# A hybrid decoder layer on one core: the decay columns of the first half in column strips, and the last level of the block inverses in quarters of the array

## The chip, the core and the metric

The kernel runs on one core of a Trainium2 chip. The metric is the device time of one execution in microseconds (us); lower is better. TensorE is called PE here, with its weight loads (PEld) shown apart; VectorE is DVE, ScalarE is ACT, GpSimd is POOL, and SyncE (SP) issues most DMAs.

## What is computed

One layer on 1024 tokens of width 2048: a combined input projection, three groups of heads, one output projection, a final RMSNorm. The part that the change touches is group B, the gated DeltaNet with 8 heads of 128. Cut to what matters:

```python
h = rmsnorm(x, ln_g)
proj = h @ w_in                      # d_a, d_b: 8 + 8 columns among 6672
g = -exp(dn_a_log) * softplus(d_a + dn_dt_bias)   # log decay per head and token
beta = sigmoid(d_b)
# per head, per chunk of the tokens
g_cum = cumsum(g)
a = strict_lower((k * beta) @ k.T * exp(g_cum_i - g_cum_j))
T = inverse(I + a)                   # unit lower triangular
v_new = T @ (beta * v) - T @ (beta * k * exp(g_cum)) @ state
```

All large products are made to nearly fp32 accuracy: each operand is split into a high and a low part in the one-pass type fp32r, and three products of the parts are added. Plain fp32 products take two PE instructions each.

## The kernel before

Tokens are worked in two halves of 512 (four tiles of 128). `h`, transposed, stands in SBUF as `ahi` and `alo` (16 row blocks k of 128 features by 512 tokens, four to a tile `q`). Weights come as pieces through `wraw` and are split into `whi` (ACT cast) and `wlo` (DVE subtraction). A product of 128 columns of `w_in` with a half is 48 matmuls of 128x512.

The order of every engine's instructions is made before anything is issued: `Plan.add` (lines 138 to 186) records each operation with its dependences, `Plan.price` gives it a cost, and `Plan.issue` (229 to 300) lets each engine take the ready operation of the lowest rank, then the oldest. Matmuls recorded in `together()` stay side by side. After a group with more than 7 followers, line 296 adds 250 ns to PE's planned time. `behind(op)` makes operations wait for `op` in the plan. All instructions carry line 300, so the trace is read by tiles.

- **Opening (lines 489 to 674).** The memory tokens' keys and values, and between them `prep(tt, put, bank)` for the tiles of the first half: scale a tile's rows (`row_scale`: four squares on ACT into `jk` and `small`, then POOL's power), transpose on PE, and `put0` (579 to 593), which splits the transposed tile into `ahq` and `alq`. For the first two tiles it makes a copy in ring `tn` first and stores that to `h0_d`.
- **First half's queries (889 to 896, called at 1247).** `project_first` makes column 0 of the queries in two parts of 256 tokens, since the last tiles are prepared late.
- **Decay columns of the first half (802 to 805, 1248 to 1252).** `decay_mm` multiplies the 32 columns `abw` (16 high parts, 16 low parts per k; read 128 wide, with 96 columns of padding) with `ahi[k]` and `alo[k]`: 32 matmuls of 128x512. `decays` (817 to 865) copies the sums, transposes them, and computes decays and betas in some 30 small operations.
- **Second half's rows (773 to 780, 1258 to 1267).** `prep1` scales and transposes the second half's tiles in place (`x_rows[4..7]`, in `ut`, `kT`, `qT`, `kd`, `ai`, `vs`, `gt`). `whole(k)` (747 to 751) adds `ahi` and `alo` of tiles 2 and 3 into `tn` and stores them to `h0_d`.
- **Second half (1274 to 1289).** The rows are split into `ahq` and `alq`; `decay_rows` (807 to 815) makes their decay columns from the unsplit rows in fp32, with the weights 32 columns wide: k mod 4 picks one of four strips of 32 output partitions, and `decays` adds the strips. `left_sums` (753 to 767) loads rows of `h0_d` back and makes sums of the halves for the later stages.
- **Main stages (1313 to 1800).** All other columns and the output projection, in sevens of block products (`seven`), with the DeltaNet's steps between. `levels` (1034 to 1116), called eight times (two halves, four pairs of heads), joins 32x32 inverses to 128x128. Its first level uses 32x32 tiles in two groups. Its last level uses four fp32 matmuls `ge` by `te` (128x128 by 128x64) and, after two ACT copies into `y2`, four of `y2` by `ue`; `ge`'s diagonal quarters are set to zero on DVE (1079, 1080), and `y2`'s unused quarters by POOL at line 1514.

Of the kernel before, what the change touches and what calls it, by code (L numbers as in the profile page):

```python
# [17 lines left out]
P = 128  # L18
# [42 lines left out]
class Plan:  # L61
# [167 lines left out]
    def issue(self):  # L229
# [11 lines left out]
        while left:  # L241
# [22 lines left out]
            for o in (head, *head.tail):  # L264
# [16 lines left out]
                for s in o.succ:  # L281
# [12 lines left out]
                    if s.n == 0:  # L294
                        heapq.heappush(soon[s.eng], (s.ready, s.idx))
            if len(head.tail) > 7:
                free[e] += self.SWITCH
# [6 lines left out]
def kernel(  # L304
# [32 lines left out]
    def C(shape, name, dt=F32):  # L337
        return sb.tile(list(shape), dt, name=name, tag=name)[:]
# [44 lines left out]
    def tok(ap):  # L383

        return ap.rearrange("p (t c) -> p t c", c=P)
# [191 lines left out]
    H0 = NT // 2  # L577

    def put0(tt):
# [12 lines left out]

        return put
# [108 lines left out]
    V.tensor_scalar(abw[:, KT * 32 :], ident[:, 0:96], 0.0, None, op0=ALU.mult)  # L702
    abv = abw[:, 0 : KT * 32].rearrange("p (k c) -> p k c", c=32)
    S.copy(abv[:, :, 0:16], abf)
# [3 lines left out]
    G.memset(halo, 0.0)  # L708
    states = C([P, NH * P], "states")
    st = [states[:, h * P : (h + 1) * P] for h in range(NH)]  # L710
# [25 lines left out]
    def over(bufs):  # L736
        r = Ring("", 0, None)
        r.bufs = bufs
        return r
# [7 lines left out]
    def whole(k):  # L747
        t = ring["tn"]()
        with rank(4):
            V.tensor_tensor(out=tok(t)[:, H0:], in0=ahi[k][:, H0:], in1=alo[k][:, H0:], op=ALU.add)  # L750
            Q.dma_start(h0_d[k][:, H0 * P :], t[:, H0 * P :])

    def left_sums(tt, q):
# [12 lines left out]
        for i, t in enumerate((d, a, c, b)):  # L766
            Q.dma_start(rows_of(s_all[i], q), tok(t))
# [24 lines left out]
    gr = C([NT * NH, P], "gr")  # L792
    y2 = C([P, 2 * NT, 64], "y2")
    steps = C([P, HT], "steps")
    spares = over([states[:, 0:HT], states[:, HT:], steps] + [t.rearrange("p c m -> p (c m)") for t in (y2, tblk)])
# [11 lines left out]
    def decay_rows(a, tt):  # L807

        with R.together():
            for q in range(NQ):  # L810
                for j in range(4):
                    k = 4 * q + j
                    PE.matmul(a[j * 32 : (j + 1) * 32, tt * P : (tt + 1) * P],
                              abw[:, k * 32 : (k + 1) * 32].bitcast(F32), tok(x_rows[NT + tt][q])[:, j],
                              start=q == 0, stop=q == NQ - 1)

    def decays(hf, a, bank):

        NU, M = NT * NH, P if hf else 32
        ab = ring["tn"]()[0:M]  # L820
        with rank(1):
            S.copy(ab, a[0:M])
        sc = scs[hf]
# [3 lines left out]
        for tt in range(NT):  # L827
            PE.transpose(tp[:, tt * M : tt * M + M], ab[:, tt * P : (tt + 1) * P], ident[0:M, 0:M])
        with rank(1):
            V.tensor_reduce(abt, tp[:, 0 : NT * M].rearrange("p (t g c) -> p t c g", t=NT, c=2 * NH), axis=AX.X, op=ALU.add)  # L830
            S.activation(beta, abt[:, :, NH:], AF.Tanh, scale=0.5)
# [202 lines left out]
    def levels(gt, tdr, udr):  # L1034
# [213 lines left out]
    a = tpb()  # L1248
    for k in range(KT):
        decay_mm(a, k)  # L1250
    marks.append(R.ops[-1])
# [28 lines left out]
    for tt in range(NT):  # L1280
        decay_rows(a, tt)
    first = project([column(0, 0), column(1, 0)], (1, 0, 2, 3))
# [24 lines left out]
    et = [heir(b, f"et{i}", tag, HT) for i, (b, tag) in enumerate(((whi.bufs[4], "whi4"), (wlo.bufs[4], "wlo4")))]  # L1307
    el = over([heir(abw, "el0", "abw", KT * 32 + 96)[:, 0:HT], ring["tn"].bufs.pop()])
    work.bufs = dnr.bufs[2:3]
# [204 lines left out]
    for u in (y2, tblk, *ring["ut"].bufs):  # L1514
        G.memset(u, 0.0)
# [315 lines left out]
```

## Time and profile before

| what | us |
|---|---|
| median of 3 runs (1599.25 to 1602.24) | 1600.16 |
| profiled execution's own time | 1599.81 |
| its span, first to last instruction | 1597.8 |
| PE busy | 1582.5 |
| DVE busy | 1314.9 |
| ACT busy | 1040.0 |
| POOL busy | 278.6 |

The span is what the trace covers; the execution has 2.0 us around it. PE's busy time counts a matmul from its start to its modelled end, and successive matmuls overlap by about 0.17 us, so what a matmul costs is read from the distance between starts. Rows of the timeline give start, duration, engine, operation, output and inputs, and in brackets how long the engine idled before and for what.

### The profile page before, as it was taken

The numbers are of one execution on the slowest core, as the hardware profiler recorded it, in microseconds if no ns is written. First come the engines' busy times: TensorE is split into PE (matmuls) and PEld (weight loads), VectorE is DVE, ScalarE is ACT, GpSimd is POOL, SyncE is SP. The second block draws the span as 40 slices with busy tenths as digits, with TensorE's granted clock in tenths as the row PEclk, the third lists the DMA queues.
The fourth block names the chain that finished last, engine by engine and source line by source line (L and its number), as shares of the span: only waits on it lengthen the run. The fifth ranks groups of instructions, "written<-read, shape, count | busy, mean of one in ns | idle before, by whom it ended". The sixth has DMA issues, their size and how long they took to land.

```text
span 1597.8 us, 26025 instructions
## 1 busy us (share of the span) xinstructions
PE 1582.5 (99%) x8580; PEld 1332.5 (83%) x8580; DVE 1314.9 (82%) x2157; ACT 1040.0 (65%) x2184; POOL 278.6 (17%) x456
## 2 busy tenths in 40 slices
PE   9999999999999999999999999999999999999997
PEld 8878888888888888888888888888888888888886
DVE  6879899869899999998988776867778788778776
ACT  7767648747755788976666667676566874344355
POOL 0101202211411412324342233032000000000001
PEclk9999999999999999999999999999999999999999
DMA  9987997897689868997789875788878879688746
GB/s 340 300 246 206 355 337 229 273 333 249 191 272 339 277 219 295 323 315 242 239 271 341 257 260 178 252 305 279 288 244 260 263 250 335 201 281 279 228 146 241
DMA packets 272744, 428.93 MB, mean 268 GB/s; under 512 B 30633, under 2 KB 97762, under 8 KB 272610
## 3 DMA queue, kind: packets, MB, share of 16 engines
q1 hardware_dynamic: 251138, 371.02, 70.9%
q0 software_dynamic: 20864, 55.20, 10.4%
q8 instruction: 67, 1.10, 0.3%
q10 hardware_dynamic: 608, 1.06, 0.2%
q14 instruction: 67, 0.55, 0.1%
HBM read 339.58 MB, written 87.06 MB: 267 GB/s over the span
## 4 chain that ended last, share of the span: by engine, by line
PE 94%; DMA 2%; ACT 1%; DVE 1%; issue 1%; SPq 0%; POOLq 0%; POOL 0%; ACTq 0%; DVEq 0%
PE acc L300 73%; PE dn L300 22%; DMA qT<-in_x_dram 0%; DMA h0d<-tn 0%; ACT whi L300 0%; DMA wraw<-in_w_in_dram 0%; DMA kvd<-vs 0%; DMA y<-h0d 0%; DMA wraw<-in_w_mem_kv_dram 0%; ACT jk L300 0%; SPq L300 0%; ACT tn L300 0%; DVE wlo L300 0%; ACT ahi L300 0%; DVE kT L300 0%
## 5 line engine op out<-in xcount | busy, mean ns | idle before, releaser
L300 PE MATMUL acc<-ahi,whi 128*128 128x512 f32 (+1 forms) x1488 | 513.4, 392 | 2.3 <-ACT ahi L300 1.1
L300 PE MATMUL acc<-ahi,wlo 128*128 128x512 f32 (+1 forms) x1040 | 404.8, 391 | 0.2 <-DVE wlo L300 0.2
L300 PEld LDWEIGHTS acc<-ahi,whi 128*128 128x128 f32 x1488 | 278.1, 188 | 57.0 <-ACT ahi L300 1.3
L300 PE MATMUL acc<-alo,whi 128*128 128x512 f32 (+1 forms) x592 | 229.2, 387 | 0.0
L300 PEld LDWEIGHTS acc<-ahi,wlo 128*128 128x128 f32 x1040 | 195.5, 188 | 37.2 <-DVE wlo L300 0.6
L300 ACT CAST ahi<-raws 128x1024 fp32r<-128x1024 f32 x148 | 155.4, 1050 | 64.0 <-PE acc L300 27.7
L300 PE MATMUL acc<-ahi,zh 128*128 128x512 f32 x448 | 176.5, 394 | 0.0
L300 PE MATMUL acc<-alo,zh 128*128 128x512 f32 x448 | 176.3, 394 | 0.0
L300 PE MATMUL acc<-ahi,zl 128*128 128x512 f32 x448 | 176.3, 394 | 0.0
L300 ACT CAST whi<-wraw 128x1024 fp32r<-128x1024 f32 (+1 forms) x116 | 108.0, 932 | 94.4 <-PE acc L300 75.6
L300 DVE TENSOR_TENSOR wlo<-wraw,whi 128x1024 fp32r<-128x1024 f32 (+1 forms) x116 | 124.2, 1073 | 38.0 <-ACT whi L300 34.4
L300 PEld LDWEIGHTS acc<-alo,whi 128*128 128x128 f32 x592 | 111.4, 188 | 20.8
L300 POOL TENSOR_TENSOR small<-small,mhalf 128x1 f32<-128x1 f32 x26 | 17.3, 672 | 525.0 <-DVE small L300 525.0
L300 DVE TENSOR_TENSOR alo<-raws,ahi 128x1024 fp32r<-128x1024 f32 x74 | 90.3, 1220 | 19.0 <-ACT ahi L300 18.4
L300 ACT CAST ahi<-y 128x1024 fp32r<-128x1024 f32 x74 | 77.7, 1049 | 40.3 <-PE dn L300 19.2
L300 DVE TENSOR_TENSOR alo<-y,ahi 128x1024 fp32r<-128x1024 f32 x74 | 90.3, 1220 | 16.1 <-ACT ahi L300 15.9
L300 DVE TENSOR_TENSOR ahi<-raws,ahi 128x1024 fp32r<-128x1024 f32 x74 | 90.4, 1222 | 15.1 <-ACT ahi L300 14.5
L300 PEld LDWEIGHTS acc<-alo,zh 128*128 128x128 f32 x448 | 84.2, 188 | 16.3
L300 PEld LDWEIGHTS acc<-ahi,zl 128*128 128x128 f32 x448 | 84.2, 188 | 16.1
L300 PEld LDWEIGHTS acc<-ahi,zh 128*128 128x128 f32 x448 | 84.2, 188 | 16.0
L300 PE MATMUL dn<-whi,ahi 128*128 128x512 f32 x224 | 77.1, 389 | 0.0
L300 PE MATMUL acc<-whi,ahi 128*128 128x512 f32 x216 | 74.9, 392 | 0.0
(464 smaller groups left out, 3451.4 us busy)
## 6 DMA issues: line engine op xcount, KB each, us to landing
wraw<-in_w_in_dram SPq DMA_DIRECT2D x224, 256.0 KB, 4.4
raws<-sa SPq DMA_DIRECT2D x128, 256.0 KB, 4.4
y<-in_w_in_dram SPq DMA_DIRECT2D x96, 256.0 KB, 4.1
y<-sa SPq DMA_DIRECT2D x64, 256.0 KB, 4.2
wraw<-in_w_out_dram SPq DMA_DIRECT2D x64, 256.0 KB, 4.4
raws<-h0d SPq DMA_DIRECT2D x62, 256.0 KB, 5.3
raws<-sd SPq DMA_DIRECT2D x44, 256.0 KB, 2.9
pd<-y SPq DMA_DIRECT2D x40, 256.0 KB, 5.2
```

What stands on the lines that cost most here:

```text
L300: o.fn(*o.args, **o.kw)
```

## The change

**Decay columns of the first half.** `decay_mm` goes; `decay_rows` now serves both halves, takes a list of (k, tile) parts, has rank 9 (before 5), and is one `together` group per call. The unsplit rows of tile 0 are kept in `raw0` (the buffers `states`, `steps` and `y2`, made earlier), those of tile 1 in that tile's own `kd` buffers, and those of tiles 2 and 3 come from `whole(k)`, which runs before the product and no longer after it. `decays` uses four strips and 128x128 transposes for both halves.

**Later loads and row scales.** `prep1` waits in the plan for the last operation of `prep(3)` (`x3`), and the first loads of `left_sums` for the last decay product (`marks[0]`).

**Last level in quarters.** The matmuls with `ge` and `y2` use only their two non-zero 64x64 quarters: 8 matmuls 64x64 by 64 in place of 4 of 128x128 by 64, one `together` group. The zeroing goes.

**Planner.** The 250 ns are added after groups with more than 6 followers.

The core of the diff:

```diff
-            if len(head.tail) > 7:
+            if len(head.tail) > 6:
                 free[e] += self.SWITCH
...
+    raw0 = [states[:, 0:HT], states[:, HT:], steps, y2.rearrange("p c m -> p (c m)")]
...
-            t = tok(ring["tn"]())
+            t = tok(x_rows[tt][q] if tt else raw0[q])
...
         prep(3, put0(3), spare)
+        x3 = R.ops[-1]
...
-    abw = C([P, KT * 32 + 96], "abw", F32R)
+    abw = C([P, KT * 32], "abw", F32R)
...
-        Q.dma_start(tok(a), rows_of(h0_d, q))
-        Q.dma_start(tok(b), rows_of(h0_d, q + 2))
+        with behind(marks[0]):
+            Q.dma_start(tok(a), rows_of(h0_d, q))
+            Q.dma_start(tok(b), rows_of(h0_d, q + 2))
...
-    def decay_mm(a, k):
-        wk = abw[:, k * 32 : k * 32 + P]
-        mm(a, wk, ahi[k], k == 0, False)
-        mm(a, wk, alo[k], False, k == KT - 1)
...
+    def decay_rows(a, parts):
+
+        with rank(9), R.together():
+            for k, x_ in parts:
+                j = k % 4
+                PE.matmul(a[j * 32 : (j + 1) * 32], abw[:, k * 32 : (k + 1) * 32].bitcast(F32), x_,
+                          start=k < 4, stop=k >= KT - 4)
...
-        with rank(1):
-            V.memset(ge[0:64, :, 0:64], 0.0)
-            V.memset(ge[64:P, :, 64:P], 0.0)
...
-        for q in range(NB // 2):
-            PE.matmul(d[:, q], ge[:, q], te[:, q], start=True, stop=True)
+        low, high = slice(0, 64), slice(64, P)
+        with R.together():
+            for q in range(NB // 2):
+                for a, b in ((low, high), (high, low)):
+                    PE.matmul(d[b, q], ge[a, q, b], te[a, q], start=True, stop=True)
...
-        for q in range(NB // 2):
-            PE.matmul(d[:, q], z[:, q], ue[:, q, 64:P], start=True, stop=True)
+        with R.together():
+            for q in range(NB // 2):
+                for a, b in ((high, low), (low, high)):
+                    PE.matmul(d[b, q], z[a, q, b], ue[a, q, high], start=True, stop=True)
...
-    for k in range(KT):
-        decay_mm(a, k)
+    for tt in range(H0):
+        decay_rows(a[:, tt * P : (tt + 1) * P], row_parts(x_rows[tt] if tt else raw0))
+    for q in range(NQ):
+        ts = [whole(4 * q + j) for j in range(4)]
+        decay_rows(a[:, H0 * P :], [(4 * q + j, t) for j, t in enumerate(ts)])
...
         for i in range(NT):
-            prep1(i)
-        for k in range(KT):
-            whole(k)
+            with behind(x3):
+                prep1(i)
```

Three places in the order of the instructions. The first is on PE, after `project_first`, where the first half's decay columns begin; `acc` are the PSUM banks, `whi`/`wlo` weights of the next projection, `abw` the decay weights. Before:

```order
L300 MATMUL acc_105<-ahi_64,whi_73 128x512
L300 MATMUL acc_105<-alo_68,whi_73 128x512
L300 MATMUL acc_105<-ahi_64,wlo_75 128x512
L300 MATMUL acc_108<-ahi_63,abw 128x512
L300 MATMUL acc_108<-alo_67,abw 128x512
```

Now:

```order
L300 MATMUL acc_105<-ahi_63,wlo_78 128x512
L300 MATMUL acc_108<-states,abw 32x128 x8
L300 MATMUL acc_108<-steps,abw 32x128 x4
L300 MATMUL acc_108<-y_130,abw 32x128 x4
L300 MATMUL acc_108<-kd_144,abw 32x128 x4
L300 MATMUL acc_108<-kd_145,abw 32x128 x4
L300 MATMUL acc_108<-kd_146,abw 32x128 x4
L300 MATMUL acc_108<-kd_147,abw 32x128 x4
L300 MATMUL acc_108<-tn_85,abw 32x256
L300 MATMUL acc_108<-tn_86,abw 32x256
L300 MATMUL acc_108<-tn_87,abw 32x256
L300 MATMUL acc_108<-tn_88,abw 32x256
```

Before, 32 such matmuls with `abw` stand nearly in a row, with two transposes of second-half rows among them. Now the parts of tiles 0 and 1 and the first four of `whole` come after 3 of the 128x512 matmuls of the next projections (before after 18), and three more groups of four `tn` follow after 14, 34 and 31 further matmuls of 128x512. The transposes of the second half's rows, which before were done by the 64th matmul of those three projections, now run on to the end of all 144; and the second half's `decay_rows`, before one row of 64 matmuls, stand in four pieces with other work between.

The second place is on ACT, at the same time: `ahi<-dn` are the casts of tile 3 of the first half, `jk,small` the squares of the second half's rows. Before:

```order
L300 ACTIVATE jk,small_103<-ut_79 128x512 x2
L300 ACTIVATE jk,small_103<-ut_80 128x512
L300 CAST ahi_63<-dn_111 128x512
L300 CAST ahi_64<-dn_112 128x512
L300 CAST whi_77<-wraw_71 128x512
L300 ACTIVATE jk,small_103<-ut_80 128x512
L300 ACTIVATE jk,small_104<-kT_388 128x512
L300 ACTIVATE jk,small_104<-kT_389 128x512
L300 CAST ahi_65<-dn_111 128x512
L300 CAST ahi_66<-dn_112 128x512
```

Now:

```order
L300 COPY xr_91<-halo 128x3
L300 CAST whi_77<-wraw_71 128x512
L300 CAST ahi_63<-dn_111 128x512
L300 CAST ahi_64<-dn_112 128x512
L300 CAST ahi_65<-dn_111 128x512
L300 CAST ahi_66<-dn_112 128x512
L300 CAST whi_73<-wraw_71 128x512
L300 ACTIVATE jk,small_103<-ut_79 128x512
```

The squares moved behind the four casts, and the cast of the next projection's first weights moved ahead of them.

The third place is on PE in the first call of `levels`: `tblk` by `gt` is the first product of the last level, `y` is `y2`. Before:

```order
L300 MATMUL dn_111<-tblk,gt_579 128x64 x4
L300 MATMUL acc_108<-ahi_63,zl 128x512
L300 MATMUL acc_106<-ahi_63,whi_74 128x512
L300 MATMUL acc_106<-alo_67,whi_74 128x512
L300 MATMUL acc_106<-ahi_63,wlo_76 128x512
```

Now:

```order
L300 MATMUL dn_111<-tblk,gt_579 64x64 x8
L300 MATMUL acc_105<-ahi_63,whi_74 128x512
L300 MATMUL acc_105<-alo_67,whi_74 128x512
L300 MATMUL acc_105<-ahi_63,wlo_76 128x512
L300 MATMUL acc_107<-ahi_63,whi_74 128x512
```

Four matmuls became eight of a quarter each, all side by side; before, the group was broken in four of its sixteen places by other small products.

More of the change, by code (lines that the diff above doesn't have):

```diff
@@ L577 @@
     H0 = NT // 2
+    states = C([P, NH * P], "states")
+    y2 = C([P, 2 * NT, 64], "y2")
+    steps = C([P, HT], "steps")
+    raw0 = [states[:, 0:HT], states[:, HT:], steps, y2.rearrange("p c m -> p (c m)")]
     def put0(tt):
@@ L699 @@
     Q.dma_start(abf, w_in[:, C_AB : C_AB + 16].rearrange("(k p) c -> p k c", p=P))
-    abw = C([P, KT * 32 + 96], "abw", F32R)
+    abw = C([P, KT * 32], "abw", F32R)
     R.users[abw.tensor.name] = []
-    V.tensor_scalar(abw[:, KT * 32 :], ident[:, 0:96], 0.0, None, op0=ALU.mult)
-    abv = abw[:, 0 : KT * 32].rearrange("p (k c) -> p k c", c=32)
+    abv = abw.rearrange("p (k c) -> p k c", c=32)
     S.copy(abv[:, :, 0:16], abf)
@@ L708 @@
     G.memset(halo, 0.0)
-    states = C([P, NH * P], "states")
     st = [states[:, h * P : (h + 1) * P] for h in range(NH)]
@@ L751, in whole @@
             Q.dma_start(h0_d[k][:, H0 * P :], t[:, H0 * P :])
+        return t[:, H0 * P :]
     def left_sums(tt, q):
@@ L792 @@
     gr = C([NT * NH, P], "gr")
-    y2 = C([P, 2 * NT, 64], "y2")
-    steps = C([P, HT], "steps")
     spares = over([states[:, 0:HT], states[:, HT:], steps] + [t.rearrange("p c m -> p (c m)") for t in (y2, tblk)])
@@ L800, with row_parts @@
     scan_banks, work = dnr.bufs[0:2], over(dnr.bufs[2:4])
-    def decay_mm(a, k):
-        wk = abw[:, k * 32 : k * 32 + P]
-        mm(a, wk, ahi[k], k == 0, False)
-        mm(a, wk, alo[k], False, k == KT - 1)
[L807 to L815, printed above, removed]
+    def decay_rows(a, parts):
[4 more added lines that the diff above has]
+                          start=k < 4, stop=k >= KT - 4)
+    def row_parts(tiles):
+        return [(4 * q + j, tok(t)[:, j]) for q, t in enumerate(tiles) for j in range(4)]
     def decays(hf, a, bank):
-        NU, M = NT * NH, P if hf else 32
-        ab = ring["tn"]()[0:M]
+        NU = NT * NH
+        ab = ring["tn"]()
         with rank(1):
-            S.copy(ab, a[0:M])
+            S.copy(ab, a)
         sc = scs[hf]
@@ L827, in decays @@
         for tt in range(NT):
-            PE.transpose(tp[:, tt * M : tt * M + M], ab[:, tt * P : (tt + 1) * P], ident[0:M, 0:M])
+            PE.transpose(tp[:, tt * P : (tt + 1) * P], ab[:, tt * P : (tt + 1) * P], ident)
         with rank(1):
-            V.tensor_reduce(abt, tp[:, 0 : NT * M].rearrange("p (t g c) -> p t c g", t=NT, c=2 * NH), axis=AX.X, op=ALU.add)
+            V.tensor_reduce(abt, tp.rearrange("p (t g c) -> p t c g", t=NT, c=2 * NH), axis=AX.X, op=ALU.add)
             S.activation(beta, abt[:, :, NH:], AF.Tanh, scale=0.5)
@@ L1280 @@
     for tt in range(NT):
-        decay_rows(a, tt)
+        decay_rows(a[:, tt * P : (tt + 1) * P], row_parts(x_rows[NT + tt]))
     first = project([column(0, 0), column(1, 0)], (1, 0, 2, 3))
@@ L1307 @@
     et = [heir(b, f"et{i}", tag, HT) for i, (b, tag) in enumerate(((whi.bufs[4], "whi4"), (wlo.bufs[4], "wlo4")))]
-    el = over([heir(abw, "el0", "abw", KT * 32 + 96)[:, 0:HT], ring["tn"].bufs.pop()])
+    el = over([heir(abw, "el0", "abw", HT), ring["tn"].bufs.pop()])
     work.bufs = dnr.bufs[2:3]
@@ L1513 @@
         early_inv = inverse([gdrs[i] for i in (0, 2, 1, 3)], "early", 1.9)
-    for u in (y2, tblk, *ring["ut"].bufs):
+    for u in (tblk, *ring["ut"].bufs):
         G.memset(u, 0.0)
```

## The prediction

> **What bounds the kernel now.** First the page: which engine is busy, and what the chain that ended last is made of.
>
> ```profile
> PE 1582.5 (99%) x8580; PEld 1332.5 (83%) x8580; DVE 1314.9 (82%) x2157; ACT 1040.0 (65%) x2184; POOL 278.6 (17%) x456
> PE 94%; DMA 2%; ACT 1%; DVE 1%; issue 1%; SPq 0%; POOLq 0%; POOL 0%; ACTq 0%; DVEq 0%
> ```
>
> PE is busy for 99% of the span, and 94% of the chain is PE. So two things count: how long PE's queue is occupied by its instructions, and where it waits in order for something. Next the list of PE's waits, which has nine rows in all; three of them here.
>
> ```profile
> PE acc L300 <- DVE kT L300: 1.2, 1, 1.2
> ...
> PE acc L300 <- ACT xr L300: 0.3, 1, 0.3
> PE acc L300 <- DVE wlo L300: 0.2, 1, 0.2
> ```
>
> The timeline places the first, and three others that bear on the change, in the opening between 71 and 90 us:
>
> ```profile
> 71.11 0.39 PE L300 MATMUL acc<-ahi,whi 128*128 128x256 f32 x1 [1.10 <-ACT ahi L300]
> 72.12 0.50 PE L300 MATMUL acc<-ahi,whi 128*128 128x512 f32 x1 [0.62 <-ACT whi L300]
> 84.47 0.50 PE L300 MATMUL acc<-ahi,abw 128*128 128x512 f32 x1 [0.47 <-DVE abw L300]
> ...
> 84.81 0.39 PE L300 MATMUL acc<-alo,abw 128*128 128x512 f32 x1
> ...
> 87.59 0.39 PE L300 MATMUL acc<-alo,abw 128*128 128x512 f32 x1
> 89.22 0.63 PE L300 MATMUL acc<-ident,kT 128*128 128x128 f32 x4 [1.24 <-DVE kT L300]
> ```
>
> The two stages are therefore different. The opening has waits to win or lose. The last two rows, 0.3 and 0.2 us, are all that the list has behind the opening; in the levels, after 700 us, the change is worth what it takes from PE's queue.
>
> All sums are made against the profiled execution, 1599.81 us with a span of 1597.8; the median of the runs is 0.35 us above it, and I make no correction for that.
>
> **Decay columns: what goes.** From 84.81 to 87.59 twelve steps take 2.78 us, 0.232 each. The 32 matmuls of 128x512 cost 32 x 0.232 = 7.4 us of PE.
>
> **What comes.** The second half's decay columns already are made in strips:
>
> ```profile
> 111.15 0.60 PE L300 MATMUL acc<-ident,gt 128*128 128x128 f32 x4
> 111.68 1.08 PE L300 MATMUL acc<-ut,abw 128*32 128x128 f32 x32
> ...
> 114.76 0.62 PE L300 MATMUL acc<-gt,abw 128*32 128x128 f32 x16
> 115.31 0.66 PE L300 MATMUL dn<-ident,qT 128*128 128x128 f32 x4
> ```
>
> and four transposes among other work take this long to the next start:
>
> ```profile
> 94.54 0.60 PE L300 MATMUL acc<-ident,kd 128*128 128x128 f32 x4
> 94.89 0.48 PE L300 MATMUL acc<-alo,whi 128*128 128x512 f32 x1
> ```
>
> From 111.68 to 115.31 is 3.63 us for four tiles, the exit included. The first half has the same columns to stream, 256 wide in tiles 2 and 3, so 3.6 us. But it comes in four groups. Entering and leaving costs: four transposes took 0.53 us up to the strips where four take 0.35 among other work (94.54 to 94.89), so 0.1 to 0.2 in; the last strips should end their issue near 115.19 (16 at 3.63/128), and the next starts 0.12 later. I take 0.2 per group beyond the first, 0.6 in all. The order shows the second half's strips cut into four pieces too: 0.6 more. So the sum is -7.4 + 3.6 + 0.6 + 0.6 = **-2.6 us**, between -3.8 (no price for cuts) and -1.4 (twice that price). The four transposes in `decays`, now of full width, cost at most these 0.35 us more, which lies within the ends; I put them at nothing, since the narrow ones were four instructions as well.
>
> **Waits of the opening that go or stay.** ACT before the wait at 71.11:
>
> ```profile
> 67.78 0.63 ACT L300 ACTIVATE jk<-ut 128x512 bf16<-128x512 f32 x1
> ...
> 70.49 1.05 ACT L300 CAST ahi<-dn 128x512 fp32r<-128x512 f32 x2
> 71.44 0.63 ACT L300 CAST whi<-wraw 128x512 fp32r<-128x512 f32 x1
> ```
>
> Three squares of second-half rows stood ahead of the cast that PE waited for; they go behind it. Alone that would free the cast at about 68.5, and 1.10 + 0.62 us could go. But the order now puts the cast `whi` ahead of `ahi`, and its load was issued late:
>
> ```profile
> 68.28 0.40 SPq L300 DMA_DIRECT2D wraw<-in_w_in_dram  x1
> wraw<-in_w_in_dram SPq DMA_DIRECT2D x224, 256.0 KB, 4.4
> ```
>
> At the median of 4.4 us from issue to landing, even an issue 1 to 2 us earlier lands near 71, so `ahi` follows at 71.5 to 72. I take these two waits as unchanged. DVE scaled four `ut` tiles ahead of `abw`, 0.75 us each, and no longer does:
>
> ```profile
> 76.51 0.75 DVE L300 SCALAR_TENSOR_TENSOR ut<-ut,small,zg 128x512 f32<-128x512 f32 x1
> ```
>
> That is 3.0 us, and PE comes to `abw` 15 matmuls earlier, 3.5 us, so that wait stays near 0.5. The 1.24 us for `kT` goes, since that transpose now stands some 40 matmuls (9 us) later. Sum **-1.3 us**; from -3.4 (all four go) to +1.5 (the weights' load holds `ahi` that much longer).
>
> **New waits.** Each of the four `tn` groups waits for four DVE additions, and those for the stores that read the same four buffers:
>
> ```profile
> 72.96 0.41 DVE L300 TENSOR_TENSOR tn<-ahi,alo 128x256 f32<-128x256 f32 x1
> 79.65 1.40 SPq L300 DMA_DIRECT2D h0d<-tn  x3
> DMA to landing us min/median/max: 1.7/5.2/8.2
> 79.72 0.40 PE L300 MATMUL acc<-ahi,wlo 128*128 128x512 f32 x1
> ```
>
> (The landing time is that of DMAs on `h0_d` up to 130 us.) Four additions take 1.6 us, a store 5.2. Behind the matmul of 79.72 PE now comes to the first group; its strips end near 82.3, and 14 matmuls later, at 85.5, the second is due. The stores that free the buffers were issued from 79.65; if that stays, they land near 85, and the second group's additions end 1 us late. Between the other groups PE has 34 and 31 matmuls, over 7 us. Behind a waiting addition on DVE stand the splits `wlo` of the next weights, so a late store reaches PE twice. I take **+1.0 us**, between 0 and 3. The reloads of `h0_d` for `left_sums`, which stood earlier in SP's order, and the two loads into `kd`, now behind the strips, need DMA room at 85 to 140 us. There is some (columns: stretch, length, busy us of PE, PEld, DVE, ACT and POOL, granted clock, busy share of the DMA engines, GB/s):
>
> ```profile
> 110.00:120.00 10.00, 10.00 (x170) 8.95 (x169) 5.54 (x12) 6.34 (x17) 0.80 (x2) 1.00 0.62 188
> ...
> 130.00:140.00 10.00, 10.00 (x46) 8.29 (x45) 10.00 (x17) 9.96 (x23) 0.00 (x0) 1.00 0.35 98
> ```
>
> **The last level.** A group of eight instructions (four products) before, and the first level's 32x32 group:
>
> ```profile
> 731.42 0.39 PE L300 MATMUL acc<-alo,zh 128*128 128x512 f32 x1
> 731.65 1.00 PE L300 MATMUL dn<-tblk,gt 128*128 128x64 f32 x8
> 732.46 0.48 PE L300 MATMUL acc<-ahi,zl 128*128 128x512 f32 x1
> ```
>
> ```profile
> 724.52 0.39 PE L300 MATMUL acc<-ahi,wlo 128*128 128x512 f32 x1
> 724.84 0.69 PE L300 MATMUL dn<-tblk,gt 32*32 32x32 f32 x32
> 725.46 0.50 PE L300 MATMUL acc<-ahi,zh 128*128 128x512 f32 x1
> ```
>
> ```profile
> 728.18 0.22 PE L300 MATMUL dn<-ut,y 32*32 32x32 f32 x2
> ...
> 728.65 0.22 PE L300 MATMUL dn<-ut,y 32*32 32x32 f32 x3
> 728.80 0.50 PE L300 MATMUL acc<-ahi,zl 128*128 128x512 f32 x1
> ```
>
> The eight take 732.46 - 731.42 = 1.04 us between the neighbours' starts, of which 0.23 belongs to the neighbour: 0.81. There are sixteen groups. The 32x32 group takes 725.46 - 724.52 = 0.94, less 0.23: 0.71, of which 0.50 is its 32 instructions and 0.2 the way in and out. The second such group (728.18 to 728.80) has 48 instructions and takes the same 0.62 from its first to its exit as the 32. So tiles in different rows and columns do work side by side: a tile issues one instruction per 0.031 us there (16 in 0.50). A 64x64 quarter has twice the columns to load and to stream, so 0.062 at most by that row, and each of the two quarters has 8: 0.50 again; 0.43 if the price follows the columns from the strips (0.109 per 128 in each strip, 0.054 per 64). I take 0.46 + 0.2 = 0.66 for a group: 16 x (0.66 - 0.81) = **-2.4 us**, with -3.2 to -1.6 as ends if the quarters overlap. The zeroing leaves DVE, where nothing waited for it:
>
> ```profile
> L300 DVE MEMSET gt<- 64x256 f32 x16 | 4.4, 272 | 1.9 <-PE dn L300 1.0
> ```
>
> It is worth nothing on the path. What the planner makes of the 250 ns now put behind the eight-transpose groups I cost at nothing: the list of waits has 0.5 us behind the opening, so the reserve there covers such shifts; if it doesn't, a late operand is worth about 1 us, as the rows of the opening show.
>
> **Sum.** 1599.8 - 2.6 - 1.3 + 1.0 - 2.4 = **1594.5 us**.
>
> **Rivals.**
>
> *The two quarters of a pair do not overlap* (10%). Both write halves of one PSUM bank; if one waits for the other, a group is 16 x 0.054 + 0.2 = 1.07 instead of 0.66, and the last level costs 16 x (1.07 - 0.81) = +4.2: 1594.5 + 2.4 + 4.2 = 1601.1, no change. Against it: the 32x32 groups also write one bank from different rows, at 0.50/32 = 0.016 per instruction where one tile alone needs 0.031. The Trainium skill, TensorEngine Tiling (Array Packing), "Restrictions and Gotchas", says that different row tiles cannot use the same PSUM bank at the same time, which would give this rival's time. By the 32x32 rows the rule does not hold as stated.
>
> *Slower: a quarter costs what a full tile costs* (5%). If loading weights into a quarter takes as long as into the whole array, and quarters follow each other, each of the 16 instructions costs 0.81/8 = 0.10, and a group 16 x 0.10 + 0.2 = 1.8: 16 x 1.0 = +16, giving 1613. The other terms give 2.9 us, so the kernel is slower by over 3.2 us once the last level costs +6.1, 0.38 per group: that is (0.81 + 0.38 - 0.2)/16 = 0.062 us per instruction. Against it speaks that the strips, with 32 columns, need 0.027 per instruction where the full array needs 0.10.
>
> *The opening takes its gain back* (20%). DVE is full at 130 to 140 us (above), and now the decay chain of the first half and the last transposes come close to the splits of the second half's rows there, where before the transposes had ended by 112. If PE waits 1 to 5 us for the last splits, the -2.9 of the opening's terms may be lost and more, and the result is 1596 to 1600. Against it: DVE was idle for nearly half of 110 to 120 us, so the chain and the splits have room if their inputs come.
>
> **How the numbers follow.** Forecast 63%, 1591 to 1597; opening 20%; no overlap 10%; full price 5%; 2% for a better result than 1590.5. The range from 1590.5 to 1601.0 takes in the forecast, the opening and about half of the no-overlap case. A measurement of this kernel can tell about 0.2%, 3.2 us, from no change. Faster by more: 0.63 + 0.02 + 0.03 (the best of the opening's cases) = 0.68. Within: 0.17 of the opening + 0.08 of no overlap = 0.25. Slower: 0.05 + 0.02 = 0.07.
>
> **What would show it.** In the changed trace: strips in the first half at 0.027 us per instruction of 128 columns and 0.054 of 256; the `kT` wait gone; the `ahi` and `whi` waits near 71 us still about 1.7 us together; sixteen groups `64*64` with 0.43 to 0.50 us from first to last start; no wait over 1 us between 100 and 180 us. A group of 0.9 or more means no overlap. A PE wait for `tn`, `alo` or `gt` in the opening means that the third rival is at work, and more than 3 us of it makes my forecast wrong.

## The result and the profile after

| | before | after |
|---|---|---|
| median of 14 runs each, us | 1599.97 (1597.37 to 1602.34) | 1604.61 (1601.22 to 1610.15) |
| after : before | | 1.0033 [1.0025, 1.0042] |
| profiled execution and its span, us | 1599.81, 1597.8 | 1606.63, 1604.6 |

The change makes the kernel 5 us slower. The forecast was 1594.5, with 1601.0 as its upper end. First the page of after: engines, and the chain that ended last.

```profile
PE 1584.3 (99%) x8772; PEld 1325.4 (83%) x8772; DVE 1303.0 (81%) x2140; ACT 1034.7 (64%) x2182; POOL 278.0 (17%) x455
PE 90%; DVE 4%; DMA 3%; ACT 1%; issue 1%; SPq 0%; POOLq 0%; POOL 0%; DVEq 0%; ACTq 0%
```

PE has 1.8 us more of busy time where the sum had 5 us less of work, and its share of the chain went from 94% to 90%, where DVE and DMA went from 3% to 7%. The list of PE's waits names what it waited for.

```profile
PE dn L300 <- DVE inv L300: 2.8, 2, 1.5
PE dn L300 <- DVE ai L300: 2.8, 2, 2.3
PE dn L300 <- issue: 1.7, 1, 1.7
PE dn L300 <- DVE whi L300: 1.5, 1, 1.5
PE dn L300 <- POOL ones L300: 1.1, 1, 1.1
PE acc L300 <- DVE alo L300: 0.9, 1, 0.9
PE acc L300 <- ACT kT L300: 0.6, 1, 0.6
PE acc L300 <- DVE xr L300: 0.5, 1, 0.5
```

The waits of before at 71 to 89 us (`kT`, `ahi`, `whi`, `abw`) are gone, and at the top stand two that before did not have: `inv` and `ai`. Both belong to the DeltaNet's step ahead of the block inverses: the buffers `inv` hold the split keys and queries there (the inverses come into the same buffers later), and `ai` takes their products times the decays. Some expectations below call them the inverses. They are no part of the opening. The table by stretches (columns as in the prediction) places them between 500 and 720 us. Before, then after:

```profile
500.00:720.00 220.00, 220.00 (x1044) 184.21 (x1043) 202.93 (x324) 176.37 (x379) 66.97 (x104) 1.00 0.87 293
```

```profile
500.00:720.00 220.00, 214.33 (x1036) 178.01 (x1034) 196.95 (x315) 171.66 (x377) 67.96 (x109) 0.99 0.85 290
```

PE was busy for all of the 220.00 us and now idles for 5.67, in a stretch where the change alters no instruction: the block inverses and the quarters come behind 720 us. Below, "PE idle" is 220 less the busy time of this row.

Two of the four waits show what happens. Here PE and, ahead of it, DVE at 640 us of after:

```profile
638.92 0.39 PE L300 MATMUL acc<-ahi,whi 128*128 128x512 f32 x1
640.76 0.50 PE L300 MATMUL dn<-inv,inv 128*128 128x256 f32 x2 [1.45 <-DVE inv L300]
```

```profile
639.34 0.69 DVE L300 TENSOR_TENSOR wraw<-wraw,qT 128x512 f32<-128x512 f32 x1 [2.52 <-DMA wraw<-in_w_in_dram]
639.95 0.17 DVE L300 COPY lhs<-hs 128x8 f32<-128x8 f32 x1
640.02 0.69 DVE L300 TENSOR_TENSOR inv<-qT,inv 128x512 fp32r<-128x512 f32 x1
```

DVE takes its instructions in order here. One of them needs a piece of weights whose load has not landed, and DVE stands still for 2.52 us. `inv`, which needs no load, is queued two places behind it, and PE waits for `inv` in turn. At 519 us the same happens behind `qT<-qT,y` (2.04 us for a load into `y`). The wait that costs most is that for `ai`, where DVE has to read a PSUM bank before PE writes it again. No load stands just before `ai`, but DVE had waited 2.96 us for one at 698.77 us and from there to `ai` worked without a pause, so it came late with all that was queued. DVE, then PE:

```profile
698.77 1.29 DVE L300 TENSOR_TENSOR kd<-kd,wraw 128x512 f32<-128x512 f32 x2 [2.96 <-DMA wraw<-in_w_in_dram]
...
709.48 0.41 DVE L300 TENSOR_TENSOR ai<-dn,E 128x256 f32<-128x256 f32 x1
```

```profile
707.29 0.39 PE L300 MATMUL acc<-ahi,whi 128*128 128x512 f32 x1
709.95 0.39 PE L300 MATMUL dn<-inv 128*128 128x256 f32 x1 [2.27 <-DVE ai L300]
...
711.09 0.63 PE L300 MATMUL acc<-ahi,whi 128*128 128x512 f32 x1
711.51 0.63 PE L300 MATMUL acc<-ahi,wlo 128*128 128x512 f32 x1
...
713.94 0.39 PE L300 MATMUL acc<-ahi,wlo 128*128 128x512 f32 x1
```

After it PE starts a 128x512 matmul every 0.43 us for a while, not every 0.23: seven of them from 711.09 to 713.94 take 2.85 us instead of 1.6. The granted clock (the column behind POOL) is half there, and 1.00 again from 714 us on:

```profile
711.00:713.00 2.00, 2.00 (x7) 1.61 (x6) 2.00 (x3) 0.00 (x0) 1.42 (x3) 0.50 0.75 233
```

So the 5.67 us of idle time cost nearly 7.

### The profile page after: what moved, and what is told of

The parts are those of the page before. It is cut to its first block, busy times and chain, and to the rows that moved or that the text cites. A ratio compares the mean times of both kernels' runs of the same rounds, so it can differ in the third digit from the quotient of the medians.

```text
span 1604.6 us, 26419 instructions
## 1 busy us (share of the span) xinstructions
PE 1584.3 (99%) x8772; PEld 1325.4 (83%) x8772; DVE 1303.0 (81%) x2140; ACT 1034.7 (64%) x2182; POOL 278.0 (17%) x455
## 4 chain that ended last, share of the span: by engine, by line
PE 90%; DVE 4%; DMA 3%; ACT 1%; issue 1%; SPq 0%; POOLq 0%; POOL 0%; DVEq 0%; ACTq 0%
PE acc L300 67%; PE dn L300 22%; DMA wraw<-in_w_in_dram 1%; DVE alo L300 1%; DMA y<-in_w_in_dram 1%; DVE wlo L300 1%; ACT y L300 0%; DMA pd<-y 0%; DMA kd<-in_x_dram 0%; DMA wraw<-in_w_mem_kv_dram 0%; DVE qT L300 0%; DVE ai L300 0%; SPq L300 0%; DVE zl L300 0%; DMA raws<-sa 0%
## 5 line engine op out<-in xcount | busy, mean ns | idle before, releaser
L300 DVE TENSOR_TENSOR alo<-y,ahi 128x1024 fp32r<-128x1024 f32 (+1 forms) x75 | 91.5, 1220 | 21.7 <-ACT ahi L300 21.2
L300 ACT CAST ahi<-y 128x1024 fp32r<-128x1024 f32 (+1 forms) x75 | 78.3, 1043 | 43.7 <-PE dn L300 19.2
L300 DVE TENSOR_TENSOR ahi<-raws,ahi 128x1024 fp32r<-128x1024 f32 x74 | 90.3, 1220 | 18.8 <-ACT ahi L300 18.5
```

The costliest lines, as they stand in the source:

```text
L300: o.fn(*o.args, **o.kw)
```

## The experiments

Theory 1 at the start was that the planner's line carries the loss, since it is the only edit that reaches the orders of that stretch; its rival was that strips or quarters do. I put the change together from its three parts: A (strips, rows kept, later loads and row scales), B (quarters), S (the planner's line alone):

```diff
-            if len(head.tail) > 7:
+            if len(head.tail) > 6:
                 free[e] += self.SWITCH
```

In the kernel before, groups with exactly 7 followers are the 24 groups of eight transposes; the changed kernel has the 16 groups of quarters besides.

**s_only, a_only, b_only, ab.**

> The kernel before with one line changed: the planner's 250 ns follow groups with more than 6 followers (it was 7). No instruction is added or taken away. Theory 1 (this line re-plans the main stages, and the waits of 0.7 to 2.4 us that the changed kernel shows at 519, 621, 640 and 710 us come from it): 4 to 8 us slower than before, 1604 to 1608, with PE waits on DVE inv or ai between 500 and 720 us. Theory 2 (the line is harmless, the strips or the quarters bring the waits): within 1.5 us of before.

> The decay columns in strips with later loads and row scales, alone; threshold and last level as before. Theory 1: -1 to -3 us, 1597 to 1599, and no wait of over 0.5 us in the main stages. Theory 2 (moving the opening shifts everything behind it): 3 us or more slower, with the waits at 500 to 720 us.

> The last level in quarters, alone; threshold and decay columns as before. Theory 1: sixteen groups save 0.11 us each as measured in the changed kernel, -1.8 us, 1598. Theory 2: the regrouped products upset the steps around them, 2 us or more slower, with new waits behind 700 us.

> Strips and quarters together, the planner's threshold as before: the changed kernel without its one-line re-planning. Theory 1: -3 to -5 us, 1595 to 1597. Theory 2: as slow as the changed kernel, 1603 to 1606.

| run | median us | against before | PE idle, 500 to 720 us |
|---|---|---|---|
| s_only | 1609.22 | 1.0064 [1.0051, 1.0078] | 3.38 |
| a_only | 1599.55 | 1.0003 [0.9995, 1.0012] | 0.63 |
| b_only | 1598.20 | 0.9996 [0.9987, 1.0005] | 0.00 |
| ab | 1599.09 | 0.9996 [0.9988, 1.0005] | 0.00 |

The line alone costs 9.7 us (1609.22 less 1599.49, the median of before in these runs), more than the whole change. Everything else in the change together costs nothing, and brings nothing that can be told from none: a_only and ab missed the ranges of 1597 to 1599 and 1595 to 1597 that theory 1 gave them. s_only has waits of after in three of the four places, at 520, 640 and 709 us:

```profile
PE dn L300 <- DVE ai L300: 1.9, 1, 1.9
PE dn L300 <- DVE inv L300: 1.5, 2, 1.1
```

(all of PE's waits between 500 and 720 us; before has none there). So the line is the cause. The question is how.

Not all of its cost is waiting. The pages of s_only and ab begin:

```profile
PE 1586.7 (99%) x8580; PEld 1333.3 (83%) x8580; DVE 1310.1 (82%) x2157; ACT 1039.8 (65%) x2184; POOL 276.7 (17%) x456
```

```profile
PE 1579.6 (99%) x8772; PEld 1321.9 (83%) x8772; DVE 1302.3 (82%) x2140; ACT 1037.7 (65%) x2184; POOL 274.2 (17%) x455
```

The line adds 9.4 us to the span of before (1607.2 for 1597.8) and 8.9 to that of ab (1604.6 in after for 1595.7). PE has the same instructions with and without it, and yet 4.2 us (1586.7 less 1582.5) and 4.7 us (1584.3 less 1579.6) of this are busy time: the same instructions take longer in the new order. The other 5.2 and 4.2 us are idle time. About 1.2 of the 4.7 is the half clock behind `ai`; the rest of the busy time was not taken apart.

**ab_own, s_125, s_500, s_less.** Theory 1 now said how: a reserve that the chip does not need is planned as idle PE, and the other engines are ordered to that slower pace. Theory 2: the reserve's size is nothing, a new order is. ab_own puts the 250 ns behind the quarters and not behind the transposes; the others change the reserve behind the 24 transposes of the kernel before.

```diff
-            if len(head.tail) > 7:
+            if len(head.tail) > 7 or head.tail and head.args[0].shape[0] == 64:
                 free[e] += self.SWITCH
```

```diff
             if len(head.tail) > 7:
                 free[e] += self.SWITCH
+            elif len(head.tail) == 7:
+                free[e] += 125.0
```

> Strips, later loads and quarters; the 250 ns stand behind the sixteen 64x64 groups and the groups with more than 7 followers, but not behind the 24 groups of eight transposes. Theory 1 (a reserve that the chip does not need is planned as idle PE, the other engines are ordered to that slower pace, and PE then waits for them; a quarter group really costs about 0.7 us where the planner prices it 0.43, so a reserve there is no idle time): as without the planner's line, 1597 to 1600. Theory 2 (any new order of everything falls as it falls, whatever the reserve): anywhere between 1597 and 1610. Theory 3 (the loss comes from the reserve behind the quarters): about 1604.

> The kernel before, with 125 ns instead of 250 behind the 24 groups of eight transposes and nothing else changed. Theory 1: a loss in proportion, about half of the 9.7 us that 250 ns cost: 1603 to 1605. Theory 2: no relation to the size; 1598 to 1610.

> The kernel before, with 500 ns behind the 24 groups of eight transposes. Theory 1: 24 x 0.5 = 12 us of planned idle time come back as waits, and some more: 1611 to 1620. Theory 2: no relation to the size; 1598 to 1610.

> The kernel before, with 250 ns taken off the planned time behind the 24 groups of eight transposes, so that the plan takes PE to be 6 us faster than it is. Theory 1: the other engines are then ordered for a PE that is faster than the real one, nothing waits that did not, 1598.5 to 1601. Theory 2: as much a new order as with 250 ns added, so 1603 to 1610 is as likely.

| run | reserve behind the 24, ns | median us | against before | PE idle, 500 to 720 us |
|---|---|---|---|---|
| ab_own | 0 | 1598.84 | 0.9998 [0.9989, 1.0006] | 0.27 |
| s_125 | 125 | 1604.51 | 1.0035 [1.0022, 1.0048] | 0.97 |
| s_500 | 500 | 1603.71 | 1.0031 [1.0019, 1.0043] | 1.01 |
| s_less | -250 | 1602.76 | 1.0021 [1.0013, 1.0030] | 1.26 |

Theory 1's "how" falls. 500 ns cost less than 250, and taking 250 away costs 3.9 us too, a time that lies between the ranges of both theories. s_125 lies in its range by chance. ab_own holds: the quarters may have the reserve.

**s_30, w_260, after_dma, no_gate.** Two smaller nudges, and two attempts at a cause. s_30 has 30 ns behind the 24 groups, 0.7 us in all. w_260 has 260 in place of 250 ns behind the groups that always had a reserve. after_dma is the whole change with a longer planned time for loads; no_gate is ab_own without the gate on the second half's row scales:

```diff
-    DMA_FIXED = 2900.0
+    DMA_FIXED = 4400.0
```

```diff
-            with behind(x3):
-                prep1(i)
+            prep1(i)
```

> The kernel before, with 30 ns behind the 24 groups of eight transposes: 0.7 us of reserve in all, and a new order on PE from about 650 us on. Theory 1 in its first form (the reserve comes back as waits in proportion): 1599 to 1600. Theory 2 (the order of before between 500 and 1250 us is one without waits, and most other orders of that stretch have some, whatever made them): 1601 to 1606.

> The kernel before, with 260 in place of 250 ns behind the groups of more than 7 followers; the order on PE is that of before up to about 700 us and another one from there to 1350. Theory 2: 1600.5 to 1605, with new waits behind 700 us. Theory 2 held to the stretch of 500 to 720 us alone, where three of the four new orders waited for the inverses: no loss, 1598.5 to 1600.

> The whole change, with the planner's time for a DMA 1.5 us longer (4400 for 2900 ns). Theory 4 (VectorE, ordered to a plan in which loads land earlier than they do, waits in order for a load, and the inverses' operations that PE needs stand behind): VectorE's waits for loads between 500 and 720 us shrink from about 10 to under 4 us, PE's four waits for inv and ai go, and the time falls to 1597.5 to 1600.5. Theory 2 (a new order falls as it falls): 1600 to 1608, with other waits.

> Strips and quarters with a reserve behind the quarters alone (as ab_own), without making the second half's row scales wait for the last tile of the first half. If that wait makes the transposes late, and so PE's waits for kT, jk, kd and xr at 90 to 160 us (4.7 us in all), these shrink to those of before and the time is 1595.5 to 1597.5. If not, the squares stand ahead of ACT's casts again (1.3 us at 71 us) and it stays at 1598 to 1600.

| run | median us | against before | DVE waits for loads, 500 to 720 us | PE idle there |
|---|---|---|---|---|
| s_30 | 1602.35 | 1.0027 [1.0016, 1.0038] | 3.5 | 0.00 |
| w_260 | 1602.68 | 1.0025 [1.0016, 1.0035] | 5.2 | 0.00 |
| after_dma | 1597.58 | 0.9989 [0.9980, 0.9999] | 2.0 | 0.00 |
| no_gate | 1597.49 | 0.9982 [0.9973, 0.9991] | 7.4 | 0.00 |

s_30 and w_260 ask the chip for nothing and lose 3 us each, so theory 2 holds: an order of the long middle is worth some us by itself, and that of before is a good one. PE has no wait between 300 and 720 us in either; w_260's largest new wait behind is this one (s_30's is 1.01 us for DVE's `tn` at 736 us):

```profile
835.05 1.21 PE L300 MATMUL dn<-ident,vs 128*128 128x128 f32 x4 [0.96 <-ACT vs L300]
```

so theory 2 held to 500 to 720 us alone falls. Again the wait is not the whole loss: w_260 has PE's order of before up to 753 us and from 1319 us on, and between the two it takes 2.3 us longer, of which 0.96 is this wait. after_dma fits theory 4 (DVE, ordered to loads that land earlier than they do) in its waits and in its time, but one kernel may be one lucky order. no_gate fits its first range, at the very edge (1597.49 for 1597.5).

**before_dma, s_dma, after_fast_dma, no_gate_dma.** The same number, 4400 for 2900, in three other kernels, and 1400 in the changed one.

> The kernel before, with the planner's time for a DMA 1.5 us longer (4400 for 2900 ns): a new order of nearly everything. Theory 4 (VectorE waits in order for loads that the plan takes to land earlier than they do): before has only 4 us of such waits between 500 and 720 us and loses nothing by them, so it stays at 1598 to 1601. Theory 2 (a new order falls as it falls, mostly worse than before): 1601 to 1606.

> The planner's line alone (as s_only, 9.7 us slower than before), with 4400 for 2900 ns. Theory 4: VectorE's waits for loads between 500 and 720 us fall from 8.7 to under 4 us, PE is idle there for under 0.5 us (3.4 in s_only), and the time is 1599 to 1603. Theory 2: 1600 to 1610 with no relation to the DMA time.

> The whole change, with the planner's time for a DMA 1.5 us shorter (1400 for 2900 ns). Theory 4: VectorE waits for more loads, 15 us and more between 500 and 720 us, PE is idle there for over 6 us, and the time is 1606 to 1620. Theory 2: 1600 to 1610, waits of VectorE as in other new orders (4 to 13 us).

> The two versions that were faster than before in one: strips, quarters with a reserve of their own, no gate for the second half's row scales, and 4400 ns for a DMA. If the two gains are of different stages, 1595 to 1597.5; if the longer DMA time only mends what the change's own planner line broke, as no_gate, 1597 to 1599; if a new order falls as it falls, 1598 to 1605.

| kernel | planned DMA time, ns | median us | against before | DVE waits for loads, 500 to 720 us | PE idle there |
|---|---|---|---|---|---|
| before | 2900 | 1599.61 | | 4.3 | 0.00 |
| before_dma | 4400 | 1606.73 | 1.0048 [1.0036, 1.0061] | 1.4 | 0.00 |
| s_only | 2900 | 1609.22 | 1.0064 [1.0051, 1.0078] | 8.7 | 3.38 |
| s_dma | 4400 | 1606.15 | 1.0039 [1.0027, 1.0051] | 2.2 | 0.00 |
| after | 2900 | 1604.61 | 1.0033 [1.0025, 1.0042] | 12.6 | 5.67 |
| after_dma | 4400 | 1597.58 | 0.9989 [0.9980, 0.9999] | 2.0 | 0.00 |
| after_fast_dma | 1400 | 1649.51 | 1.0312 [1.0297, 1.0327] | 18.5 | 9.68 |
| no_gate | 2900 | 1597.49 | 0.9982 [0.9973, 0.9991] | 7.4 | 0.00 |
| no_gate_dma | 4400 | 1604.99 | 1.0032 [1.0020, 1.0044] | 3.1 | 0.00 |

(The medians are of several comparisons, each with its own runs of before; the ratios take that out.) For the time as a whole theory 4 fails: three of the four kernels with the longer time are slower than before, before_dma and s_dma missed its ranges, and after_fast_dma lies 30 us beyond. For its stretch it holds in all four: DVE's waits for loads fall below 3.2 us, and PE is idle for 0.00 us wherever it was idle. The opposite change does the opposite, and PE waits more throughout the main stages; after_fast_dma between 500 and 720 us:

```profile
500.00:720.00 220.00, 210.32 (x987) 173.52 (x986) 193.59 (x323) 173.51 (x385) 67.40 (x107) 0.99 0.84 292
```

The new losses with 4400 ns stand elsewhere: in before_dma 3.0 us for DVE's `tn` at 743 us and 1.3 for ACT's `whi` at 212, in s_dma 2.3 for `whi` at 208 and 1.5 for DVE's `states` at 752, in no_gate_dma six waits of 0.6 to 1.7 us at 120 to 140 us. The long time had ordered the opening anew as well.

**after_stage, s_stage.** So the last two leave the opening as it was:

```diff
-                    done = (dma if e == "sp" else max(dma, beside[e])) + self.DMA_FIXED + o.lat
+                    done = (dma if e == "sp" else max(dma, beside[e])) + self.DMA_FIXED + (1500.0 if o.at > 250000.0 else 0.0) + o.lat
```

> The whole change, with 1.5 us more for a DMA in the plan, but only for those planned after 250 us, so that the opening stays that of the change. Theory 4, held to the stretch of 500 to 720 us: VectorE's waits for loads there fall from 12.6 to under 4 us and PE's idle time from 5.7 to under 0.3 us, and the time from 1604.6 to 1597.5 to 1600.5. Theory 2: PE idle there for 1 to 4 us as in other new orders, 1600 to 1608.

> The planner's line alone, with the same 1.5 us for DMAs planned after 250 us. Theory 4, held to that stretch: VectorE's waits for loads there fall from 8.7 to under 4 us, PE's idle time from 3.4 to under 0.3 us, and of the 9.7 us of s_only 3.4 and what follows from them are won back: 1602 to 1606, with what it lost behind 720 us left to chance. Theory 2: PE idle for 1 to 4 us, no gain.

| run | median us | against before | DVE waits for loads, 500 to 720 us | PE idle there |
|---|---|---|---|---|
| after_stage | 1597.78 | 0.9992 [0.9983, 1.0000] | 1.3 | 0.00 |
| s_stage | 1601.61 | 1.0011 [1.0001, 1.0020] | 0.0 | 0.00 |

after_stage has, between 500 and 720 us, no PE wait at all, and of DVE's waits for loads one line is left where after had five:

```profile
DVE wraw L300 <- DMA wraw<-in_w_in_dram: 3.8, 3, 2.5
DVE kd L300 <- DMA wraw<-in_w_in_dram: 3.0, 1, 3.0
DVE kT L300 <- DMA wraw<-in_w_in_dram: 2.9, 2, 2.1
...
DVE qT L300 <- DMA y<-in_w_in_dram: 2.0, 1, 2.0
...
DVE y L300 <- DMA y<-in_w_in_dram: 0.9, 1, 0.9
```

```profile
DVE wraw L300 <- DMA wraw<-in_w_in_dram: 1.3, 1, 1.3
```

(after first, then after_stage.) after_stage fell into the range of theory 4 and not into that of theory 2; s_stage came out 0.4 us better than theory 4 gave. In the changed kernel 6.8 us are won back, about the 5.67 us of idle time and the slow matmuls behind it, although a new wait of 2.24 us (DVE's `states`) came at 747 us. With the line alone 7.6 are won back, where only 3.38 us were idle in the stretch: so the new order behind 250 us did more there than end these waits.

How far such figures go without a new order can be read from seven kernels whose engines all have the same order in this stretch (before, a_only, b_only, ab, ab_own, w_260, no_gate): DVE's waits for loads come to 4.3 to 7.8 us there and PE's idle time to 0.00 to 0.63. After (12.6 and 5.67), after_fast_dma (18.5 and 9.68) and s_only (8.7 and 3.38) lie above both ranges; s_125, s_500 and s_less, with 0.97 to 1.26 us of idle time, are a little above the second. The six traces with a longer planned time for loads lie below the first, at 0.0 to 3.1 us.

**A version that beats both.** no_gate is the fastest against its own runs of before, by 0.18% (0.09 to 0.27); as the best of eighteen versions it may owe some of that to chance. It needs no figure of the planner but a reserve for the quarters. What it still loses is one wait in the opening:

```profile
87.81 0.63 PE L300 MATMUL acc<-ident,kT 128*128 128x128 f32 x4 [3.13 <-DVE kT L300]
```

```profile
86.31 0.69 DVE L300 TENSOR_TENSOR wlo<-wraw,whi 128x512 fp32r<-128x512 f32 x1 [3.71 <-ACT whi L300]
86.92 1.41 DVE L300 SCALAR_TENSOR_TENSOR kT<-kT,small,zg 128x512 f32<-128x512 f32 x2
```

```profile
85.66 0.62 ACT L300 CAST whi<-wraw 128x512 fp32r<-128x512 f32 x1 [3.39 <-DMA wraw<-in_w_in_dram]
```

It is the same pattern: a late load holds ACT's cast, the cast holds DVE's `wlo`, and `kT`, which needs neither, stands behind `wlo`.

## Why the prediction was wrong

**The step that failed is the last sentence of the part on the last level**: that the planner's 250 ns cost nothing, because "the list of waits has 0.5 us behind the opening, so the reserve there covers such shifts". A list without waits is no reserve: it says that this order fits, not that another would. The term put at nothing measured 5.5 us in the changed kernel (by the medians, 1604.61 for ab's 1599.09) and 9.7 us in the kernel before; without it the time lies inside the stated range, 4.6 us above the forecast. The slack that the argument needed could have been looked up in the trace of before: DVE's list of waits between 500 and 720 us, with 4.3 us for loads, among them this line:

```profile
DVE kd L300 <- DMA wraw<-in_w_in_dram: 1.2, 1, 1.2
```

That is, DVE already ran into loads in this stretch, without reaching PE (4.3 to 7.8 us in the seven kernels with this order). The change makes it 12.6 us, and PE is reached. Its other half, that "a late operand is worth about 1 us", was short as well: the four waits of after come to 5.6 us, and the longest slowed PE behind it. I had taken the line for an edit to 24 groups; in s_only it changes the order of ACT from 118 us on and that of PE from 164 us on, both up to about 1331 us.

**Decay columns, forecast -2.6: right to half a us.** The first half's strips in after:

```profile
79.37 0.40 PE L300 MATMUL acc<-ahi,wlo 128*128 128x512 f32 x1
79.69 0.65 PE L300 MATMUL acc<-states,abw 128*32 128x128 f32 x16
...
81.47 0.61 PE L300 MATMUL acc<-tn,abw 128*32 128x256 f32 x8
82.01 0.50 PE L300 MATMUL acc<-ahi,whi 128*128 128x512 f32 x1
...
85.09 0.39 PE L300 MATMUL acc<-alo,whi 128*128 128x512 f32 x1
85.41 0.64 PE L300 MATMUL acc<-tn,abw 128*32 128x256 f32 x8
85.98 0.51 PE L300 MATMUL acc<-ahi,wlo 128*128 128x512 f32 x1
```

The first group takes 82.01 - 79.37 - 0.23 = 2.41, a lone `tn` group 85.98 - 85.09 - 0.23 = 0.66, three of them 1.98: 4.4 us, where I had 4.2 with the first half's cuts. The 64 instructions of 128 columns from 79.69 to 81.47 take 0.028 each, as expected. The second half's four pieces take 4.64 us by the same measure, where its one piece of before took 3.63 and 0.18 for the way in: 0.8 for the cuts, where I had 0.6. Together -7.4 + 4.4 + 0.8 = -2.2. (The way out was read too short from the rows of before: the last strip there starts at 115.11 us and the next instruction 0.20 later, where I had 115.19 and 0.12.)

**Opening, forecast -1.3 and +1.0: the balance of about nothing is right in after, by other waits than I named, and 1.3 to 2.5 us off in ab, ab_own and a_only.** PE's waits from 60 to 300 us are 4.2 us before, 3.7 after, 5.2 in ab, 6.2 in ab_own and 6.4 in a_only. The `kT` wait of before went, as forecast, and those for `ahi`, `whi` and `abw` went as well, which I had as staying. In a_only came `kT` on ACT 1.4, `xr` 1.3, `alo` 0.9, `ai` 1.4 and 1.1 of issue; no wait for `tn` came in the opening. After has one of 1.65 us at 177 us, where I had said that none over 1 us would come. In a_only the +2.2 us of waits are as much as the strips bring, and the time is that of before. This is the third rival's time, at the upper end of its range, but only in part its mechanism: of the waits that were to show it only `alo` came, 0.9 us, and the others are for ACT's `kT` and `xr`, for `ai` and for issue. no_gate shows that the gate on the row scales makes most of them: without it none of these is longer than 0.2 us, its waits are 3.7 us (3.1 of them a new one for DVE's `kT`) where ab_own has 6.2, and by the ratios it is 0.16%, 2.6 us, faster than ab_own, though the two intervals touch.

**Last level, forecast -2.4: the mechanism right, the term too large.** A group of quarters in after:

```profile
728.95 0.39 PE L300 MATMUL acc<-ahi,whi 128*128 128x512 f32 x1
729.27 0.68 PE L300 MATMUL dn<-ut,y 64*64 64x64 f32 x16
729.88 0.50 PE L300 MATMUL acc<-alo,whi 128*128 128x512 f32 x1
```

The quarters overlap: 16 instructions from 729.27 to the last start at 729.73, 0.46, as forecast. The way in and out is 0.24 (729.88 - 728.95 - 0.23 - 0.46) for 0.2, so a group costs 0.70 and not 0.66; and the four groups that before had broken by other products were the cheaper ones. By rows it comes to about -1.7. So the rival without overlap, and with it the rule of the Trainium skill that was weighed there (TensorEngine Tiling (Array Packing), "Restrictions and Gotchas"), gave the wrong time, and so did the rival of the full price. The way in and out of 0.24 us agrees with what the Trainium skill says in TensorEngine Tiling (Array Packing), "Key Properties": "Mode switching requires drain".

With the terms as measured, ab should gain 2.2 + 1.7 - 1.0 = 2.9 us; it gains 0.6 (-0.8 to 1.9). At least 1 us of that I can't place; in the one profiled pair PE's busy time does fall by 2.9 us (1579.6 for 1582.5) and the span by 2.1.

**What stays open.** Waits of PE explain only a part of what a new order costs. PE's busy time for the same 8580 instructions is 1582.5 us in before and 1583.3 to 1586.7 in the six kernels whose reserve alone was changed (s_less 1583.3, w_260 1583.8, s_125 1584.1, s_30 1584.5, s_500 1585.4, s_only 1586.7); which neighbours make it longer was only seen, not taken apart. And I have not shown why the order that comes from the line makes DVE meet more late loads than that of before; only that planned load times settle how many it meets.

## What to carry to other kernels

Where a planner makes the order, an edit to its prices is an edit to the stages behind, and its cost is not the size of the number: 30 ns cost 3 us here and 500 ns no more than 125. Price such an edit by how many us a new order has cost, and keep it from stages that the rest of the change leaves alone (a reserve for the new groups only: 1598.84 for 1604.61). Before counting on slack, read the waits of the engine that feeds the bottleneck too: an engine that takes its queue in order and waits for a load holds up everything behind it, even what needs no load.

## What the hardware showed that I had not expected

PE's half pace after a wait. Of the eight waits of more than 2.2 us behind the first 60 us of all the traces, seven were followed by a stretch at a granted clock of 0.50 that began 0.3 us before to 1.6 us after the wait's end and lasted 3.41 us, with 128x512 matmuls 0.43 us apart (after_stage 2.24, s_dma 2.26, after 2.27, after_fast_dma 2.90 and 3.97, before_dma 3.05, no_gate 3.13 us; one of 2.60 in after_fast_dma was not). Of the 45 waits between 1.0 and 2.2 us only five were followed by such a stretch (one of them of 6.83 us), the shortest 1.33 us. The Trainium skill, TensorE: Matmul & The Clock Gate, "What's actually happening", says that the clock is at half after an idle window of about 3.4 us, and that the window runs by itself. The 3.41 us of the stretches here agree with that length, and a window that runs by itself would explain why no single length of a wait decides; that a wait of 1.33 to 2.3 us can be enough is not what it says. The start-to-start of 426.7 ns that the Trainium skill gives for the cold array in TensorE: Matmul & The Clock Gate, "Wait — 56ns, not 53.3ns?", agrees with the 0.43 here.

A group of eight instructions of 32x256 strips costs 0.66 us by itself, of which 0.31 pass between the start of its last instruction and the next matmul; behind 128-column strips that way out is 0.20 us, and behind quarters 0.15.
